# Gate and up projections multiplied in blocks: seven block products in place of eight, from the third chunk of inner features on

## The chip, the cores and the metric

The kernel runs on one core of one Trainium2 chip. A core has a matmul engine (PE, whose weight loads are listed as PEld), a vector engine (DVE), a scalar engine (ACT), a general engine (POOL) and a queue engine (SP), and each works through its own instructions in order; they meet at semaphores. Operands lie in an on-chip memory of 128 partitions (SBUF), and matmul results in 8 accumulator banks of 128 by 512 fp32 values (PSUM). The metric is the time of one execution in device microseconds (us): 2798.61 before, the median of 3 runs that lie between 2798.51 and 2798.78.

## The reference

A decoder trunk of 2 layers, over 512 tokens of 1024 features. Each layer is a gated feed-forward block (FFN), a block of three parallel token mixers, and a second FFN. The change touches the first half of the four FFNs only, the products with `w_gate` and `w_up`:

```
D_MODEL = 1024;  SEQ = 512;  DEPTH = 2;  D_FF = 2816
def swiglu(x, w_gate, w_up, w_down):
    return (jax.nn.silu(x @ w_gate) * (x @ w_up)) @ w_down
...
y = swiglu(rms_norm(h, ffn1_pre_g[l]), ffn1_w_gate[l], ffn1_w_up[l], ffn1_w_down[l])
h = h + MACARON_WEIGHT * rms_norm(y, ffn1_post_g[l])
```

All is fp32, and the kernel keeps nearly that precision: every operand of a matmul is split into a rounded part and the remainder, and three matmuls (hi by hi, hi by lo, lo by hi) make one product.

## The kernel before

**The products.** The normalised input stands transposed in SBUF as `xhi` and `xlo`, 8 blocks of 128 features by 512 tokens each. The 2816 inner features are worked off in 11 chunks of 256. For each chunk `load` (L220) brings 1 MB of `w_gate` and 1 MB of `w_up` into two staging buffers `ws`, one each, so a chunk's load waits until the last reader of the same matrix's earlier chunk is done. `part` and `split` (L201, L202) make the two halves of a piece of weights: ACT casts the rounded part `wh`, then DVE subtracts it from the weights to leave `wl`. There are three buffers each for `wh` and `wl`, of 128 by 1024.

**A chunk.** The first chunk of each FFN is multiplied the other way round: a tile of 128 tokens is the stationary operand and 256 columns of weights stream through (`gate_up`, its first loop). Meanwhile the last token tiles of the stage before are still being normalised and transposed into `xhi`, `xlo` (`spread`, called through `catch_up`). From the second chunk on weights are stationary and 512 tokens stream. Each 128 inner features take 8 feature blocks by 3 matmuls for gate and as many for up, so one chunk is 2 x 2 x 8 x 3 = 96 matmuls of 512 columns (`mm3`, L244 to L246). Then ACT applies silu to the gate sums (L1094) and DVE multiplies by the up sums (L1095) into `hid`, which `down` splits and multiplies with `w_down`.

**What sets the order.** A scheduler orders the instructions of each engine when the program is built; at run time each engine takes its own list strictly in order. Pools rotate: 7 buffers of 128 by 512 (`t`), 4 of 128 by 1024 (`m`), the three of `wh` and `wl`, and 8 banks.

The two functions that the diff touches, and what calls them:

Of the kernel before, what the change touches and what calls it, by code (L numbers as in the profile page):

```python
# [11 lines left out]
F32 = mybir.dt.float32  # L12
F32R = mybir.dt.float32r
I32 = mybir.dt.int32
AF = mybir.ActivationFunctionType
# [5 lines left out]
P = 128  # L21
# [4 lines left out]
KD = D // P  # L26
# [24 lines left out]
for _n, _k in (("ident", P), ("tri", P), ("ones64", P), ("ones", P),  # L51
# [8 lines left out]
BANKS = {"pj": (0, 1), "a": (2, 3, 4), "z": (5,), "n": (6,), "y": (7,), "all": tuple(range(8)),  # L60
         "t0": (0, 1), "t1": (2, 3), "t2": (4, 5), "t3": (6, 7)}

PUMP = {
# [35 lines left out]
class Core:  # L101
# [137 lines left out]
        for s in range(cols // P):  # L239
            yield self.part(st[:, :, s * P:(s + 1) * P])  # L240

    def mm3(self, out, whi, wlo, xhi, xlo, start, stop):
        nc = self.nc
        nc.tensor.matmul(out, whi, xhi, start=start, stop=False)  # L244
        nc.tensor.matmul(out, whi, xlo, start=False, stop=False)  # L245
        nc.tensor.matmul(out, wlo, xhi, start=False, stop=stop)  # L246

    def proj(self, ps, w, xhi, xlo, kc=KD):
        wh, wl = w
# [811 lines left out]
class Trunk(Rwkv, Hgrn, Mla, Core):  # L1061
    def gate_up(self, l, n):
        nc = self.nc
        hid = Lazy(lambda i: self.slot((0, 1, 2, 5, 8, 9)[i]))
        wg, wu = self.a[f"ffn{n}_w_gate"][l], self.a[f"ffn{n}_w_up"][l]

        g, u = self.first or (self.load(wg, KD, 256), self.load(wu, KD, 256))
        self.first = None
        gs = [self.part(g[:, 4 * i:4 * i + 4]) for i in range(2)]
        us = [self.part(u[:, 4 * i:4 * i + 4], (10, 9 if n == 1 else 7)[i]) for i in range(2)]  # L1070
        for t in range(NT):
            tk = slice(t * P, (t + 1) * P)
            ps = self.psum(f"t{t}", (P, 2, 256))
            for i, w in enumerate((gs, us)):
                for k in range(KD):
                    n = KD // len(w)
                    wh, wl = w[k // n]
                    self.mm3(ps[:, i], self.xhi[:, k, tk], self.xlo[:, k, tk], wh[:, k % n], wl[:, k % n], k == 0, k == KD - 1)
            sg = self.t2(shape=(P, 256))
            nc.scalar.activation(sg, ps[:, 0], AF.Silu)  # L1080
            nc.vector.tensor_mul(sg, sg, ps[:, 1])  # L1081
            ps = self.psum(f"t{t}", (P, 2, P))
            for i in range(2):
                self.transpose(ps[:, i], sg[:, i * P:(i + 1) * P])
            nc.scalar.copy(hid[0][:, 0:2, tk], ps)
            self.catch_up()
        for c in range(1, FF // 256):
            for s, (g, u) in enumerate(zip(self.columns(wg, KD, 256, col0=c * 256), self.columns(wu, KD, 256, col0=c * 256))):
                f = 2 * c + s
                pg, pu = self.psum("all"), self.psum("all")  # L1090
                self.proj(pg, g, self.xhi, self.xlo)
                self.proj(pu, u, self.xhi, self.xlo)
                sg = self.t2()
                nc.scalar.activation(sg, pg, AF.Silu)  # L1094
                nc.vector.tensor_mul(hid[f // 4][:, f % 4, :], sg, pu)  # L1095
        return hid


    def rows(self, acc, half, t, w, x, first, last):
# [209 lines left out]
```

## Time and profile before

| | |
|---|---|
| median of 3 runs | 2798.61 us |
| the profiled execution's own time | 2810.86 us |
| its span, first to last instruction | 2809.0 us |
| PE busy, share of the span | 2761.9 us, 98% |
| DVE busy | 1365.5 us, 49% |
| ACT busy | 1165.5 us, 41% |
| mean granted PE clock | 0.989 |
| HBM traffic over the span | 109 GB/s |

The profiled execution takes 12 us longer than the median of the plain runs. Its rows give durations and distances within it. Matmul rows overlap: the time from the start of one to the start of the next is what one costs in a stream, and the row's own length is longer. A row's columns in the timeline are start, length, engine, line, operation, operands (result before the arrow), and the idle time before it with what ended it. In rows of groups, the count stands after x, then busy us in total and the mean ns of one.

### The profile page before, as it was taken

Reading aid. Unit: us, or ns where it says so; the run is one execution under the profiler, and the core shown is the slowest. Engines: PE = TensorE matmul, PEld = TensorE weight load, DVE = VectorE, ACT = ScalarE, POOL = GpSimd, SP = SyncE. Lnnn points to the kernel's source line nnn. Section 1 sums busy time; section 2 is a strip of 40 time slices with the busy share of each in tenths; the row PEclk is TensorE's granted clock in tenths of the full one; section 3 lists DMA queues with packets and bytes.
Section 4 is the critical chain, followed back from the end, with each engine's and each line's share of the span. In section 5 each row is a group of like instructions: output and inputs, shape, how many; then the busy total and the mean of one; then the engine's idle time right before and its main releaser. Section 6 shows DMA issues by size and latency. Waiting matters only on the chain. (4 is left out here: it accounts for less than half of the span.)

```text
span 2809.0 us, 36592 instructions
## 1 busy us (share of the span) xinstructions
PE 2761.9 (98%) x15077; PEld 2271.6 (81%) x15077; DVE 1365.5 (49%) x2075; ACT 1165.5 (41%) x1901; POOL 59.0 (2%) x121
## 2 busy tenths in 40 slices
PE   8999999989999999999999999999899999999999
PEld 7888887777887888888888888877778878888887
DVE  3223347763866662223432233467558576522333
ACT  3223347345657542222332233364465584422232
POOL 0000010000000010000000000100000000100000
PEclk9999999899999999999999999999999999999999
DMA  4322332324421552322313233333253325323322
GB/s 164 103 97 92 119 118 94 104 70 160 147 79 63 173 176 83 105 90 98 127 63 103 90 105 112 103 106 103 83 195 102 106 68 179 131 90 97 102 102 75
DMA packets 223490, 307.32 MB, mean 109 GB/s; under 512 B 11856, under 2 KB 181052, under 8 KB 221788
## 3 DMA queue, kind: packets, MB, share of 16 engines
q1 hardware_dynamic: 223324, 304.99, 32.8%
q8 instruction: 118, 1.93, 0.3%
q14 instruction: 48, 0.39, 0.0%
HBM read 269.84 MB, written 35.13 MB: 109 GB/s over the span
## 5 line engine op out<-in xcount | busy, mean ns | idle before, releaser
L201 ACT CAST wh<-ws 128x1024 fp32r<-128x1024 f32 (+4 forms) x484 | 431.8, 902 | 1144.7 <-PE b L245 853.8
L246 PE MATMUL b<-xhi,wl 128*128 128x512 f32 x2176 | 857.8, 394 | 0.0
L244 PE MATMUL b<-xhi,wh 128*128 128x512 f32 x2176 | 856.8, 394 | 0.0
L245 PE MATMUL b<-xlo,wh 128*128 128x512 f32 x2176 | 856.2, 393 | 0.0
L202 DVE TENSOR_TENSOR wl<-ws,wh 128x1024 fp32r<-128x1024 f32 (+4 forms) x484 | 497.8, 1037 | 543.2 <-ACT wh L201 533.3
L244 PEld LDWEIGHTS b<-xhi,wh 128*128 128x128 f32 x2176 | 410.4, 189 | 89.8 <-issue 5.1
L246 PEld LDWEIGHTS b<-xhi,wl 128*128 128x128 f32 x2176 | 410.6, 189 | 87.4 <-issue 3.0
L245 PEld LDWEIGHTS b<-xlo,wh 128*128 128x128 f32 x2176 | 410.5, 189 | 86.1 <-issue 3.2
L244 PE MATMUL b<-wh,t 128*128 128x512 f32 x576 | 227.3, 395 | 0.0
L245 PE MATMUL b<-wl,t 128*128 128x512 f32 x576 | 227.3, 395 | 0.0
L246 PE MATMUL b<-wh,t 128*128 128x512 f32 x576 | 227.3, 395 | 0.0
L1095 DVE TENSOR_TENSOR s<-t,b 128x512 f32<-128x512 f32 x80 | 55.1, 688 | 265.9 <-PE b L246 265.9
L202 DVE TENSOR_TENSOR t<-s,t 128x512 fp32r<-128x512 f32 x80 | 54.6, 691 | 176.6 <-PE b L245 169.1
L245 PEld LDWEIGHTS b<-wl,t 128*128 128x128 f32 x576 | 108.5, 188 | 25.5
L246 PEld LDWEIGHTS b<-wh,t 128*128 128x128 f32 x576 | 108.5, 188 | 25.4
L244 PEld LDWEIGHTS b<-wh,t 128*128 128x128 f32 x576 | 108.5, 188 | 25.1
L244 PE MATMUL b<-s,wh 128*128 128x512 f32 x256 | 100.1, 391 | 0.0
L245 PE MATMUL b<-s,wh 128*128 128x512 f32 x256 | 99.6, 389 | 0.0
L246 PE MATMUL b<-s,wl 128*128 128x512 f32 x256 | 99.6, 389 | 0.0
L244 PE MATMUL b<-s,s 128*128 128x512 f32 x192 | 75.6, 394 | 0.0
L246 PE MATMUL b<-s,s 128*128 128x512 f32 x192 | 74.9, 390 | 0.0
L245 PE MATMUL b<-s,s 128*128 128x512 f32 x192 | 74.8, 390 | 0.0
(304 smaller groups left out, 3393.1 us busy)
## 6 DMA issues: line engine op xcount, KB each, us to landing
ws<-in_w_in_dram SPq DMA_DIRECT2D x58, 1024.0 KB
ws<-in_ffn_w_up_dram SPq DMA_DIRECT2D x44, 1024.0 KB
ws<-in_ffn_w_down_dram SPq DMA_DIRECT2D x44, 1024.0 KB
ws<-in_ffn_w_gate_dram SPq DMA_DIRECT2D x43, 1024.0 KB
gd<-f SPq DMA_DIRECT2D x48, 256.0 KB
t<-gd SPq DMA_DIRECT2D x48, 256.0 KB
s<-cd SPq DMA_DIRECT2D x8, 1024.0 KB
ws<-in_w_o_dram SPq DMA_DIRECT2D x8, 1024.0 KB
```

The costliest lines, as they stand in the source:

```text
L201: self.nc.scalar.copy(hi, src)
L202: self.nc.vector.tensor_sub(lo, src, hi.bitcast(F32))
L244: nc.tensor.matmul(out, whi, xhi, start=start, stop=False)
L245: nc.tensor.matmul(out, whi, xlo, start=False, stop=False)
L246: nc.tensor.matmul(out, wlo, xhi, start=False, stop=stop)
L1095: nc.vector.tensor_mul(hid[f // 4][:, f % 4, :], sg, pu)
```

## The change

From the third chunk on, a chunk is treated as a product of two 2 by 2 block matrices. The input is cut by tokens (two halves of 256) and features (two halves of 512): A11, A12, A21, A22, where A12 is the first token half with the second feature half. The weights are cut by features, with gate and up side by side: `b11` and `b21` are the upper and lower half of the gate columns, `b12` and `b22` those of the up columns. Strassen's scheme, in the form with 7 products and shared sums, gives gate and up of both token halves from seven block products. Each has 512 features, 256 inner features and 256 tokens: 2 x 4 x 3 = 24 matmuls of 256 columns, so a chunk has 7 x 24 = 168 of these in place of 96 of 512.

Sums of input blocks are formed once per FFN, in `token_sums`: 8 DVE additions or subtractions and 4 splits, all of 128 by 1024; S1, S2 and S4 go into slots of their own and S3 overwrites the block A21. Per chunk `seven` adds 4 subtractions of weight blocks on DVE (t1, t2, t3, and t2 again), splits seven pieces of weights in place of four, copies three banks to SBUF on ACT, adds three results and multiplies two on DVE, and takes two silus on ACT.

```diff
+PLAIN = 2
...
         for c in range(1, FF // 256):
-            for s, (g, u) in enumerate(zip(self.columns(wg, KD, 256, col0=c * 256), self.columns(wu, KD, 256, col0=c * 256))):
...
+            if c < PLAIN:
...
+            else:
+                if c == PLAIN:
+                    A = self.token_sums()
+                self.seven(A, self.load(wg, KD, 256, col0=c * 256), self.load(wu, KD, 256, col0=c * 256),
+                           hid[c // 2][:, 2 * (c % 2):2 * (c % 2) + 2, :])
         return hid
+
+    def token_sums(self):
+        nc = self.nc
+        U = (slice(0, 256), slice(256, 512))
+        at = lambda i, j: (self.xhi[:, 4 * j:4 * j + 4, U[i]], self.xlo[:, 4 * j:4 * j + 4, U[i]])
+        whole = lambda hi, lo: (hi.bitcast(F32), lo.bitcast(F32))
+        S = {"A11": at(0, 0), "A12": at(0, 1), "A22": at(1, 1)}
+        a, b, c = [self.m4((P, 4, 256)) for _ in range(3)]
+        add, sub = nc.vector.tensor_add, nc.vector.tensor_sub
+        add(a, *whole(*at(1, 0)))
+        add(b, *whole(*at(1, 1)))
+        add(b, a, b)
+        add(c, *whole(*at(0, 0)))
+        sub(a, c, a)
...
+        put("S1", 6, b)
+        sub(b, b, c)
+        put("S2", 7, b)
+        add(c, *whole(*at(0, 1)))
+        sub(c, c, b)
+        put("S4", 10, c)
+        self.split(*at(1, 0), a)
+        S["S3"] = at(1, 0)
+        return S
+
+    def seven(self, S, g, u, dst):
+        nc = self.nc
+        b11, b21, b12, b22 = g[:, 0:4], g[:, 4:8], u[:, 0:4], u[:, 4:8]
+        sub = nc.vector.tensor_sub
+        ps = [self.psum("all", (P, 2, 256)) for _ in range(3)]
+        started = set()
+
+        def product(i, w, x):
+            wh, wl = self.part(w)
+            xh, xl = S[x]
+            for s in range(2):
+                f = slice(s * P, (s + 1) * P)
+                for k in range(4):
+                    self.mm3(ps[i][:, s], wh[:, k, f], wl[:, k, f], xh[:, k], xl[:, k], i not in started, s == 1 and k == 3,
+                             skip_group_check=True)
+                    started.add(i)
+
+        def keep(i):
+            x = self.t2(shape=(P, 2, 256))
+            nc.scalar.copy(x, ps[i])
+            return x
+
+        product(0, b11, "A11")
+        t1, t2, t3 = [self.m4((P, 4, 256)) for _ in range(3)]
+        sub(t1, b12, b11)
+        p1 = keep(0)
+        product(1, t1, "S1")
+        sub(t2, b22, t1)
+        p5 = keep(1)
+        product(0, t2, "S2")
+        v = keep(0)
+        sub(t3, b22, b12)
+        product(2, b21, "A12")
+        nc.vector.tensor_add(p1, p1, ps[2])
+        nc.scalar.activation(p1, p1, AF.Silu)
+        product(0, t3, "S3")
+        nc.vector.tensor_add(p5, p5, ps[0])
+        product(1, b22, "S4")
+        nc.vector.tensor_add(v, v, ps[1])
+        nc.vector.tensor_mul(dst[:, :, 0:256], p1, v)
+        sub(t2, b21, t2)
+        product(0, t2, "A22")
+        sg = self.t2(shape=(P, 2, 256))
+        nc.scalar.activation(sg, ps[0], AF.Silu)
+        nc.vector.tensor_mul(dst[:, :, 256:512], sg, p5)
```

**How rows move.** A program lists each engine's instructions in the order in which the engine takes them. Names are those of the buffers: `wh`, `wl` the halves of a piece of weights, `ws` the staged weights, `m` a sum of weight blocks, `t` a buffer of 128 by 512, `b` a bank, `s` a slot (here a part of `hid`). In the changed kernel L205 is the second half of a split, L1167, L1170, L1174 and L1183 the four subtractions of weights, L1181 the addition that completes an up result, L1182 and L1187 the two multiplications into `hid`.

DVE in the middle of an FFN, one chunk before:

```order
L202 TENSOR_TENSOR wl_688<-ws_685,wh_687 128x1024
L202 TENSOR_TENSOR wl_694<-ws_691,wh_693 128x1024
L1095 TENSOR_TENSOR s_82_622<-t_682,b_88_633 128x512
L202 TENSOR_TENSOR wl_751<-ws_685,wh_750 128x1024
L202 TENSOR_TENSOR wl_755<-ws_691,wh_754 128x1024
L1095 TENSOR_TENSOR s_82_622<-t_747,b_97_698 128x512
```

and the first 12 of the 16 instructions of a chunk now (the other four are the split of `b22`, L1176, the split of the seventh piece, and L1179):

```order
L205 TENSOR_TENSOR wl_1262<-ws_1254,wh_1261 128x1024
L1167 TENSOR_TENSOR m_1289<-ws_1256,ws_1254 128x1024
L1181 TENSOR_TENSOR t_1130<-t_1130,b_136_1035 128x512
L1170 TENSOR_TENSOR m_1290<-ws_1256,m_1289 128x1024
L1182 TENSOR_TENSOR s_134_1033<-t_1069,t_1130 128x2x256
L205 TENSOR_TENSOR wl_1296<-m_1289,wh_1295 128x1024
L205 TENSOR_TENSOR wl_1327<-m_1290,wh_1326 128x1024
L1187 TENSOR_TENSOR s_134_1033<-t_1251,t_1100 128x2x256
L1174 TENSOR_TENSOR m_1291<-ws_1256 128x1024
L205 TENSOR_TENSOR wl_1358<-ws_1254,wh_1357 128x1024
L1183 TENSOR_TENSOR m_1290<-ws_1254,m_1290 128x1024
L205 TENSOR_TENSOR wl_1388<-m_1291,wh_1387 128x1024
```

Splits of the next chunk (`ws_1254`) now stand between the additions and multiplications that finish the chunk before it (`b_136_1035`, `s_134_1033`).

ACT where the gate and up products of an FFN end and `down` begins. Before, with the last silu at L1094 and the first two splits of `hid` behind it:

```order
L201 CAST wh_1743<-ws_1709 128x1024
L1094 ACTIVATE t_1694<-b_219_1644 128x512
L201 CAST t_1715<-s_47_262 128x512
L201 CAST t_1747<-s_47_262 128x512
L201 CAST t_1781<-s_47_262 128x512
```

and now, with the last silu at L1186:

```order
L204 CAST wh_2615<-ws_2613 128x1024
L204 CAST wh_2647<-ws_2613 128x1024
L204 CAST wh_2681<-ws_2679 128x1024
L1186 ACTIVATE t_2598<-b_294_2381 128x512
L204 CAST t_2619<-s_47_262 128x512
L204 CAST t_2651<-s_47_262 128x512
```

In both, the splits of `hid` that `down` needs first stand behind a silu. That silu reads the bank of the last-but-one product before (the gate product, with the up product still to follow), and the bank of the last product now. The same rows stand at this place in all four FFNs.

DVE in the second FFN, from the last token tile's transposes (`xlo`) to the third chunk; before:

```order
L202 TENSOR_TENSOR xlo_81<-b_1338_8500,xhi_80 128x4x128
L1081 TENSOR_TENSOR t_8556<-t_8556,b_1339_8507 128x256
L202 TENSOR_TENSOR wl_8628<-ws_8625,wh_8627 128x1024
L202 TENSOR_TENSOR wl_8685<-ws_8619,wh_8684 128x1024
L1081 TENSOR_TENSOR t_8612<-t_8612,b_1342_8563 128x256
L202 TENSOR_TENSOR wl_8689<-ws_8625,wh_8688 128x1024
```

and now (L1117 to L1131 are additions of `token_sums`, L1084 is the multiplication that was L1081):

```order
L205 TENSOR_TENSOR xlo_81<-b_1434_9404,xhi_80 128x4x128
L1117 TENSOR_TENSOR m_9649<-xhi_80,xlo_81 128x1024
L1118 TENSOR_TENSOR m_9650<-xhi_80,xlo_81 128x1024
L1120 TENSOR_TENSOR m_9651<-xhi_80,xlo_81 128x1024
L1119 TENSOR_TENSOR m_9650<-m_9649,m_9650 128x1024
L1121 TENSOR_TENSOR m_9649<-m_9651,m_9649 128x1024
L1084 TENSOR_TENSOR t_9460<-t_9460,b_1435_9411 128x256
L205 TENSOR_TENSOR s_1460_9657<-m_9650,s_1460_9657 128x1024
L205 TENSOR_TENSOR wl_9532<-ws_9529,wh_9531 128x1024
L1129 TENSOR_TENSOR m_9650<-m_9650,m_9651 128x1024
L205 TENSOR_TENSOR wl_9589<-ws_9523,wh_9588 128x1024
L1131 TENSOR_TENSOR m_9651<-xhi_80,xlo_81 128x1024
```

Five additions of the token sums now stand between the last `xlo` and the third tile's multiplication, and further sums between the splits of the second chunk's weights. Outside the four gate and up stages and their borders, the lists of all engines read as before. On SP one thing moves: the loads of the gain vectors for the norms behind the FFN (512 KB each, into `m` buffers, L264 now) stood ahead of most gate and up loads and now stand behind the last of them, just ahead of the first load of `w_down`.

More of the change, by code (lines that the diff above doesn't have):

```diff
@@ L240, in columns, with mm3 @@
             yield self.part(st[:, :, s * P:(s + 1) * P])
-    def mm3(self, out, whi, wlo, xhi, xlo, start, stop):
+    def mm3(self, out, whi, wlo, xhi, xlo, start, stop, **kw):
         nc = self.nc
-        nc.tensor.matmul(out, whi, xhi, start=start, stop=False)
-        nc.tensor.matmul(out, whi, xlo, start=False, stop=False)
-        nc.tensor.matmul(out, wlo, xhi, start=False, stop=stop)
+        nc.tensor.matmul(out, whi, xhi, start=start, stop=False, **kw)
+        nc.tensor.matmul(out, whi, xlo, start=False, stop=False, **kw)
+        nc.tensor.matmul(out, wlo, xhi, start=False, stop=stop, **kw)
     def proj(self, ps, w, xhi, xlo, kc=KD):
@@ L1087, in gate_up @@
         for c in range(1, FF // 256):
-            for s, (g, u) in enumerate(zip(self.columns(wg, KD, 256, col0=c * 256), self.columns(wu, KD, 256, col0=c * 256))):
[L1089 to L1095, printed above, removed]
@@ L1096, in gate_up @@
-        return hid
+            if c < PLAIN:
+                for s, (g, u) in enumerate(zip(self.columns(wg, KD, 256, col0=c * 256), self.columns(wu, KD, 256, col0=c * 256))):
+                    f = 2 * c + s
+                    pg, pu = self.psum("all"), self.psum("all")
+                    self.proj(pg, g, self.xhi, self.xlo)
+                    self.proj(pu, u, self.xhi, self.xlo)
+                    sg = self.t2()
+                    nc.scalar.activation(sg, pg, AF.Silu)
+                    nc.vector.tensor_mul(hid[f // 4][:, f % 4, :], sg, pu)
+            else:
[3 more added lines that the diff above has]
+                           hid[c // 2][:, 2 * (c % 2):2 * (c % 2) + 2, :])
@@ new lines, in gate_up, with put @@
+        return hid
+    def token_sums(self):
[11 more added lines that the diff above has]
+        sub(a, c, a)
+        def put(name, i, x):
+            both = self.slot(i, (P, 2, 4, 256), F32R)
+            self.split(both[:, 0], both[:, 1], x)
+            S[name] = both[:, 0], both[:, 1]
+        put("S1", 6, b)
[7 more added lines that the diff above has]
+        return S
```

## The prediction

> **What bounds the kernel now.** I read the page's first part and the waits of PE first.
>
> ```profile
> PE 2761.9 (98%) x15077; PEld 2271.6 (81%) x15077; DVE 1365.5 (49%) x2075; ACT 1165.5 (41%) x1901; POOL 59.0 (2%) x121
> ...
> PE b L516 <- DVE m L499: 16.7, 2, 8.5
> PE b L197 <- DVE m L282: 9.1, 3, 8.3
> PE b L197 <- DVE t L1081: 3.3, 3, 1.9
> ```
>
> PE is occupied nearly throughout, and its longest waits (us in total, times, longest) lie in the mixers (L516) and at the borders of stages. No wait of the gate and up chunks is among them. So these chunks cost what their matmuls cost, and DVE and ACT have room. The queue's own list gives the period of a chunk: each chunk issues one load of gate weights.
>
> ```profile
> 66.68 0.37 SPq L220 DMA_DIRECT2D ws<-in_ffn_w_gate_dram  x1
> 72.12 0.37 SPq L220 DMA_DIRECT2D ws<-in_ffn_w_up_dram  x1
> 88.44 0.37 SPq L220 DMA_DIRECT2D ws<-in_ffn_w_gate_dram  x1
> ...
> 131.96 0.37 SPq L220 DMA_DIRECT2D ws<-in_ffn_w_gate_dram  x1
> ```
>
> From 66.68 to 88.44 is 21.76 us, and from 66.68 to 131.96 three times that. A chunk has 96 matmuls, so one costs 21.76/96 = 226.7 ns. The timeline shows the same spacing, start to start, also while ACT and DVE split weights beside it:
>
> ```profile
> 102.42 1.05 ACT L201 CAST wh<-ws 128x1024 fp32r<-128x1024 f32 x1 [4.38 <-PE b L245]
> 102.45 0.39 PE L244 MATMUL b<-xhi,wh 128*128 128x512 f32 x1
> 102.67 0.39 PE L245 MATMUL b<-xlo,wh 128*128 128x512 f32 x1
> ...
> 103.51 1.23 DVE L202 TENSOR_TENSOR wl<-ws,wh 128x1024 fp32r<-128x1024 f32 x1 [4.21 <-ACT wh L201]
> ...
> 104.49 0.39 PE L244 MATMUL b<-xhi,wh 128*128 128x512 f32 x1
> ```
>
> Nine matmuls start between 102.45 and 104.49: 2.04/9 = 226.7 ns. The row's own 0.39 us is latency and overlaps the next row.
>
> **The matmuls after the change.** The question is what a matmul of 256 columns costs; half of 226.7 would be 113.3. The first chunk of each FFN runs such a stream already, with a 128 by 128 weight load for each matmul and the same three-matmul pattern:
>
> ```profile
> 30.29 0.28 PE L246 MATMUL b<-wh,xlo 128*128 128x256 f32 x1
> ...
> 30.31 0.38 ACT L1080 ACTIVATE t<-b 128x256 f32<-128x256 f32 x1 [1.00 <-PE b L246]
> ...
> 30.73 0.42 DVE L1081 TENSOR_TENSOR t<-t,b 128x256 f32<-128x256 f32 x1 [2.34 <-ACT t L1080]
> ...
> 31.01 0.28 PE L246 MATMUL b<-wh,xlo 128*128 128x256 f32 x1
> ...
> 33.28 0.28 PE L244 MATMUL b<-s,xhi 128*128 128x256 f32 x1
> 33.28 0.19 PEld L245 LDWEIGHTS b<-s,xhi 128*128 128x128 f32 x1
> ...
> 36.16 0.28 PE L244 MATMUL b<-wh,xhi 128*128 128x256 f32 x1
> ```
>
> From 33.28 to 36.16 are 24 starts: 120.0 ns each; from 30.29 to 31.01, with ACT and DVE at work, six at 120 too. So 512 columns cost 226.7 and 256 cost 120.0: 256 columns of streaming are 106.7 and each matmul has a fixed 13.3 on top. Seven eighths of the multiplications therefore cost 168 x 0.120 = 20.16 us a chunk and not 7/8 of 21.76 (19.04). **A chunk gains 1.60 us**, and nine chunks in each of four FFNs gain 36 x 1.60 = **57.6 us**. No gain is left where the spacing exceeds 21.76/168 = 129.5 ns, so there are 9.5 ns of room.
>
> The Trainium skill, page "TensorE: Matmul & The Clock Gate", section "Back-to-back issue gap", has two rules here. For a matmul alone it gives columns/2.4 + 2.5 ns: by it a chunk would go from 96 x 215.8 = 20.7 to 168 x 109.2 = 18.3 us, and the sum would gain 85. For a stream of weight loads and matmuls it gives 81 ns at 128 columns and 131 at 512; taking 98 between them as an estimate, a chunk would go from 12.6 to 16.4 us, and the change would cost 139 us. This case's 226.7 ns at 512 columns agrees with neither, and the second speaks against the change; the rows decide.
>
> **DVE and ACT beside them.** The rows by form that price the new work:
>
> ```profile
> L202 DVE TENSOR_TENSOR wl<-ws,wh 128x1024 fp32r<-128x1024 f32 x364 | 444.6, 1224 | 510.8 <-ACT wh L201 502.8
> L1095 DVE TENSOR_TENSOR s<-t,b 128x512 f32<-128x512 f32 x80 | 55.1, 688 | 265.9 <-PE b L246 265.9
> L201 ACT CAST wh<-ws 128x1024 fp32r<-128x1024 f32 x364 | 382.6, 1052 | 1074.6 <-PE b L245 785.8 <-PE b L246 251.3 <-issue 15.7
> L201 ACT CAST t<-s 128x512 fp32r<-128x512 f32 x80 | 48.5, 616 | 0.0
> L256 ACT COPY f<-b 128x512 f32<-128x512 f32 x82 | 47.5, 580 | 4.9 <-issue 4.4 <-PE b L246 0.3
> L1094 ACT ACTIVATE t<-b 128x512 f32<-128x512 f32 x80 | 47.3, 592 | 0.0
> ```
>
> DVE had 4 splits and 2 multiplications a chunk, 6.3 us. It gets 7 splits, 4 subtractions and 5 operations of 512: 11 x 1.224 + 5 x 0.688 = 16.9 us, 84% of 20.16. ACT gets 7 x 1.052 + 3 x 0.580 + 2 x 0.592 = 10.3 us. Both fit beside PE in sum; whether they fit in order needs DVE's list. I count from the end of the fifth product (S3) of a chunk. DVE then adds (0.69), splits the next chunk's b11 (1.22), forms t1 (1.22), adds v (0.69; its product ended at 2.88), forms t2 (1.22), multiplies (0.69) and splits t1 (1.22): 6.9 us. PE has three products of 24 x 0.12 = 2.88 us to do until it takes t1, at 8.6. The reserve is 1.7 us, the smallest of the seven; t2 comes at 8.1 for 11.5. So a steady chunk loses nothing by it; the price if the cover goes is under the rivals.
>
> **Weights.** The next loads may start when `b21` and `b22` were read last. From t1's subtraction to the split of b22 DVE has 9 operations of 1.224 and 3 of 0.688, 13.1 us. A load needs, by the windows around the issues at 66.68 and 72.12 (last two columns: share of the DMA engines, GB/s):
>
> ```profile
> 66.00:68.00 2.00, 2.00 (x11) 1.65 (x10) 0.65 (x1) 0.00 (x0) 0.00 (x0) 1.00 0.11 20
> 68.00:70.00 2.00, 2.00 (x10) 1.69 (x9) 0.00 (x0) 0.22 (x1) 0.00 (x0) 1.00 0.94 300
> 70.00:72.00 2.00, 2.00 (x10) 1.65 (x9) 1.13 (x1) 1.33 (x2) 0.00 (x0) 1.00 0.59 204
> 72.00:74.00 2.00, 2.00 (x11) 1.65 (x10) 0.09 (x1) 0.00 (x0) 0.00 (x0) 1.00 0.34 89
> ```
>
> The first ends before 72, so under 5.3 us. The loop is at most 18.4 of 20.16 us, closed with 1.8 to spare. The gain vectors that move on SP wait only for the last chunk's t1, which is split before `w_down` may load; I cost that at nothing.
>
> **Token sums.** 12 operations of 1.224 on DVE, 14.7 us an FFN. Uncovered they would cost 4 x 14.7 = 59 us, all of the gain. Their cover, in the second FFN:
>
> ```profile
> 1059.80 1.29 DVE L202 TENSOR_TENSOR xlo<-b,xhi 128x512 fp32r<-128x512 f32 x2 [0.16 <-ACT xhi L201]
> 1066.28 0.42 DVE L1081 TENSOR_TENSOR t<-t,b 128x256 f32<-128x256 f32 x1 [5.20 <-ACT t L1080]
> ...
> 1072.39 0.42 DVE L1081 TENSOR_TENSOR t<-t,b 128x256 f32<-128x256 f32 x1 [1.05 <-ACT t L1080]
> ```
>
> Inputs are whole at 1061.1, and the third chunk starts one chunk (21.8) after about 1072, at 1094: 33 us. DVE has 12 sums and splits, the second chunk's 4 splits, and for the third chunk 2 splits and 3 subtractions: 21 x 1.224, with small ones 28 us. They fit. But five sums now stand ahead of the third tile's multiplication, which starts at 1067.2, not 1066.28, and more ahead of the fourth, which slips to 1073.8 (five more operations of 1.224 behind 1067.6). PE's list lets nine matmuls of the second chunk (2 us) pass before that tile's transposes. Between 0 and 1.5 us an FFN I take **0.5, in all 2 us**.
>
> **The way into `down`.** Now the splits of `hid` that `down` takes first stand on ACT behind the silu of the last product. Before:
>
> ```profile
> 255.75 0.59 ACT L1094 ACTIVATE t<-b 128x512 f32<-128x512 f32 x1
> 256.24 1.65 ACT L201 CAST t<-s 128x512 fp32r<-128x512 f32 x3
> ```
>
> those casts were done by 257.9, and `down` began at 260.21 without a gap:
>
> ```profile
> 259.98 0.40 PE L246 MATMUL b<-xhi,wl 128*128 128x512 f32 x1
> 260.21 0.40 PE L244 MATMUL b<-wh,t 128*128 128x512 f32 x1
> ```
>
> Now PE ends its last product, ACT needs 0.59 for the silu and 0.62 for the cast, with some 0.15 for the result to reach ACT (latency 0.28 against a spacing of 0.12): 1.36 us in which PE has nothing else in its list. The remainder that DVE forms is needed seven matmuls later (1.6 us) and ready by then. Bounds 0.6 and 3 us; I take 1.36, **four times 5.4 us**.
>
> **Sum.** 57.6 - 2 - 5.4 = 50 us less. The profiled execution would go from its span of 2809.0 to 2759 (2810.86 to 2761); the gain is PE time in a stream, so the plain median goes from 2798.6 to **2748**.
>
> **Rivals.** *DVE's list sets the chunk, slower.* Its 16.9 us leave 3.3 idle in a chunk, and five of its sixteen operations wait for a result of PE or ACT, with the next chunk's splits queued behind. If it must stand for more than 21.76 - 16.9 = 4.9 us a chunk, nothing is gained. Two waits as long as a product, 5.8, give 22.7 us: 36 x 0.9 = 32 us more, with the borders 2838. One wait of 4.1 us gives 21.0, 30 us lost, and 2778. For it speaks the 84%, against it the reserves above: each result is ready when DVE comes to it.
>
> *Weight loads no longer hide, slower.* A load row lasts 0.19 us and the stream gives it 0.12, so loads overlap. If they did not when ACT and DVE load the memory, 168 x 0.19 = 31.9 us a chunk and a time near 3171; it decides from 129.5 ns on. Against it: 120 in rows with ACT and DVE busy, if lightly. (The stream rule of the Trainium skill's page "TensorE: Matmul & The Clock Gate" points the same way.)
>
> *The fixed part vanishes.* 113.3 ns, 36 x 2.72 = 98 us, about 2708. Nothing in the first chunk speaks for it. (The same page's rule for a matmul alone, with its 2.5 ns, comes near this one.)
>
> *The token sums are not covered.* 59 us lost, no change: 2799. Against it the 33 us of cover.
>
> **How the numbers follow.** Forecast 0.78, around 2748; DVE in part, near 2778, 0.08; DVE in full, 2838, 0.05; loads that don't hide 0.03; no fixed part 0.03; no change 0.03. Under the forecast alone 2740 (no losses at the borders, 57.6 gained) to 2760. To hold eight in ten I take 2738 to 2780, upwards because the unpriced part, DVE at 84%, can only cost. A measurement of this kernel tells 0.2% (5.6 us) from no change: faster 0.89, same 0.03, slower 0.08.
>
> **What would show it.** Gate loads 20.16 us apart in the steady chunks; matmul starts 120 ns apart there; DVE busy about 16.9 us of each chunk, yet no PE wait for a split; a PE gap of 1 to 2 us ahead of `down`, ended by ACT's cast; mixers unchanged. Wrong would be a spacing above 125 ns, PE waits for `wl` or `wh` in each chunk, or a gap of several us where the third chunk begins.

## The result, and the profile after

| | median, us | runs | profiled execution (span) | mean granted clock |
|---|---|---|---|---|
| before | 2798.68 | 2798.51 to 2798.78 | 2810.86 (2809.0) | 0.989 |
| after | 2751.32 | 2750.68 to 2752.31 | 2752.31 (2750.4) | 0.992 |

The ratio is 0.983, 95% interval [0.981, 0.984]: the change saves 47.4 us, and 2748 (50 us less) had been predicted, in a range of 2738 to 2780. The profiled spans differ by more, 58.6 us. A part of that is the clock. One minus the mean clock, times the span, is 30.9 us of lost cycles before and 22.0 after; the stretches at half clock that make the difference lie in the mixers, which the change doesn't touch (the longest, 27.3 us from 532.9 us on, stands in the execution before only).

The page of after begins with the busy times:

```profile
PE 2695.3 (98%) x17669; PEld 2341.1 (85%) x17669; DVE 1773.3 (64%) x2483; ACT 1347.5 (49%) x2133; POOL 58.5 (2%) x121
```

PE has 2592 matmuls more and is busy 66.6 us less. DVE has 408 us more to do, almost all of it beside PE. Whether that holds chunk by chunk is read from the queue's own list (one gate load a chunk) and from windows cut at two of these loads. Window columns: the stretch and its length, then busy time and instructions of PE, PEld, DVE, ACT and POOL, granted clock, DMA share, GB/s.

```profile
1097.78 0.37 SPq L223 DMA_DIRECT2D ws<-in_ffn_w_gate_dram  x1
1117.94 0.37 SPq L223 DMA_DIRECT2D ws<-in_ffn_w_gate_dram  x1
1138.11 0.37 SPq L223 DMA_DIRECT2D ws<-in_ffn_w_gate_dram  x1
...
1198.58 0.37 SPq L223 DMA_DIRECT2D ws<-in_ffn_w_gate_dram  x1
```

```profile
1097.78:1117.94 20.16, 20.16 (x171) 20.16 (x170) 16.06 (x16) 9.83 (x13) 0.00 (x0) 1.00 0.33 105
1117.94:1138.11 20.17, 20.17 (x171) 20.17 (x170) 16.07 (x16) 9.84 (x13) 0.00 (x0) 1.00 0.33 106
```

Six loads stand between 1097.78 and 1198.58, five steps of 20.16 us, as forecast, and PE is busy in every one of those microseconds at full clock. The waits of PE, by total:

```profile
PE b L519 <- DVE m L502: 16.6, 2, 8.5
PE b L200 <- DVE m L285: 9.0, 4, 8.1
PE b L247 <- ACT t L204: 8.1, 4, 2.0
PE b L200 <- DVE t L1084: 2.9, 3, 1.9
```

The mixers' wait (L519, before L516) is as it was, and so is the one ahead of the first chunk (L200 for L285). The wait for the first chunk's multiplication (L1084, before L1081), which the token sums were to make longer, went from 3.3 us to 2.9. No wait of a steady chunk is in the list. One row is new: four times 2.0 us for ACT's cast `t`. That is the way into `down`. Here it is in the first FFN, PE and ACT together:

```profile
245.25 0.28 PE L248 MATMUL b<-xlo,wh 128*128 128x256 f32 x1
245.37 0.28 PE L249 MATMUL b<-xhi,wl 128*128 128x256 f32 x1
245.57 1.04 ACT L204 CAST wh<-ws 128x1024 fp32r<-128x1024 f32 x1 [1.78 <-PE b L248]
246.52 0.59 ACT L1186 ACTIVATE t<-b 128x512 f32<-128x512 f32 x1
247.01 1.13 ACT L204 CAST t<-s 128x512 fp32r<-128x512 f32 x2
247.67 0.50 PE L247 MATMUL b<-wh,t 128*128 128x512 f32 x1 [2.02 <-ACT t L204]
```

From PE's last matmul of the stage (245.37) to the first of `down` (247.67) are 2.30 us. Before, that step was 0.23 (259.98 to 260.21 in the prediction's rows), so it is 2.07 us longer. Against the 0.12 that a stream of 256 columns gives it, each border costs 2.18 us, where 1.36 had been counted. The row that was not counted is the third one: a cast of weights for `down` that waits 1.78 us and stands ahead of the silu.

After the gap the clock fell in two of the four FFNs. Windows at the start of `down` in the first and the second FFN:

```profile
248.50:251.90 3.40, 3.40 (x10) 2.64 (x9) 2.98 (x5) 2.18 (x4) 0.00 (x0) 0.50 0.30 123
1255.40:1258.90 3.50, 3.50 (x10) 2.75 (x9) 3.13 (x6) 2.18 (x4) 0.00 (x0) 0.51 0.35 145
```

At a clock of 0.50, 3.4 us hold half of the matmuls that they could. `down` took 101.81 and 102.21 us in these two FFNs by its matmul starts, 100.25 in the other two, and 100.16 in all four before: 3.7 us in sum for the two.

Why two of four can be read from the kept traces. Seven traces, this one and those of six experiments below, have this gap, in 28 places, and half clock followed at 15 of them; at the 24 ways into `down` of the six traces without it (the kernel before among them) it never did. In each trace the half-clock stretches begin at whole multiples of 3.413 us from one another (the two here 1006.93 us, 295 times 3.4133). Divide the execution into such intervals: at the 15 places 1.88 to 2.02 us of the gap lie in the one interval ahead of the half clock, at the 13 others the border of two intervals cuts the gap and neither holds more than 1.85. So the gap brings the half clock, and where it happens to lie on that grid decides whether it does.

### The profile page after: what moved, and what is told of

It reads as the page before. It is cut to its first block, busy times and chain, and to the rows that moved or that the text cites. A ratio compares the mean times of both kernels' runs of the same rounds, so it can differ in the third digit from the quotient of the medians.

```text
span 2750.4 us, 42564 instructions
## 1 busy us (share of the span) xinstructions
PE 2695.3 (98%) x17669; PEld 2341.1 (85%) x17669; DVE 1773.3 (64%) x2483; ACT 1347.5 (49%) x2133; POOL 58.5 (2%) x121
## 5 line engine op out<-in xcount | busy, mean ns | idle before, releaser
L249 PE MATMUL b<-xhi,wl 128*128 128x256 f32 (+1 forms) x2176 | 734.0, 337 | 0.0
L247 PE MATMUL b<-xhi,wh 128*128 128x256 f32 (+1 forms) x2176 | 734.0, 337 | 0.0
L248 PE MATMUL b<-xlo,wh 128*128 128x256 f32 (+1 forms) x2176 | 732.6, 337 | 0.0
L204 ACT CAST wh<-ws 128x1024 fp32r<-128x1024 f32 (+4 forms) x448 | 393.5, 889 | 676.8 <-PE b L248 295.8
L205 DVE TENSOR_TENSOR wl<-ws,wh 128x1024 fp32r<-128x1024 f32 (+4 forms) x448 | 453.2, 1021 | 271.0 <-ACT wh L204 265.9
L247 PEld LDWEIGHTS b<-xhi,wh 128*128 128x128 f32 x2176 | 414.7, 191 | 45.2 <-issue 4.9
L248 PEld LDWEIGHTS b<-xlo,wh 128*128 128x128 f32 x2176 | 414.9, 191 | 40.8 <-issue 2.6
L247 PE MATMUL b<-s,wh 128*128 128x256 f32 (+1 forms) x1120 | 344.6, 308 | 0.0
L248 PE MATMUL b<-s,wh 128*128 128x256 f32 (+1 forms) x1120 | 344.2, 307 | 0.0
L249 PE MATMUL b<-s,wl 128*128 128x256 f32 (+1 forms) x1120 | 344.1, 307 | 0.0
L204 ACT CAST wh<-m 128x1024 fp32r<-128x1024 f32 x144 | 151.3, 1050 | 232.4 <-PE b L248 98.1
L248 PE MATMUL b<-wl,t 128*128 128x512 f32 x576 | 228.6, 397 | 0.0
L247 PEld LDWEIGHTS b<-s,wh 128*128 128x128 f32 x1120 | 213.9, 191 | 10.9 <-DVE s L991 1.2
L249 PEld LDWEIGHTS b<-s,wl 128*128 128x128 f32 x1120 | 213.9, 191 | 10.1
L248 PEld LDWEIGHTS b<-s,wh 128*128 128x128 f32 x1120 | 214.0, 191 | 9.8
L205 DVE TENSOR_TENSOR wl<-m,wh 128x1024 fp32r<-128x1024 f32 x144 | 173.8, 1222 | 34.2 <-ACT wh L204 34.2
L205 DVE TENSOR_TENSOR t<-s,t 128x512 fp32r<-128x512 f32 x80 | 54.9, 690 | 176.9 <-PE b L248 158.9
```

Of the source, the lines that this page charges most:

```text
L204: self.nc.scalar.copy(hi, src)
L205: self.nc.vector.tensor_sub(lo, src, hi.bitcast(F32))
L247: nc.tensor.matmul(out, whi, xhi, start=start, stop=False, **kw)
L248: nc.tensor.matmul(out, whi, xlo, start=False, stop=False, **kw)
L249: nc.tensor.matmul(out, wlo, xhi, start=False, stop=stop, **kw)
```

## Experiments

The theory after the comparison (Theory 1): PE alone sets the chunks, with 120 ns for a matmul of 256 columns whatever stands beside it; DVE's added work lies beside PE until DVE is full (after t3 was formed three times this became: what counts is that each result is ready when PE takes it, which depends on the place of an operation in DVE's list); what was lost is the border into `down`, where PE waits for ACT. Rivals: the 120 ns hold a loss by DVE's and ACT's load on the memory; DVE's sum of work is what limits; the border has little part in the missing microseconds.

| kernel | median, us | ratio to before, 95% interval |
|---|---|---|
| after | 2751.3 | 0.983 [0.981, 0.984] |
| first split of `hid` ahead of the last product | 2742.7; again 2742.2 | 0.980 [0.978, 0.982]; 0.980 [0.978, 0.982] |
| the kernel before, products in two halves of 256 columns | 2845.2 | 1.016 [1.015, 1.018] |
| scheme from the seventh chunk on | 2777.1 | 0.992 [0.990, 0.994] |
| without the subtractions of weights | 2758.2 | 0.984 [0.981, 0.987] |
| t3 three times (2 more DVE operations a chunk) | 2767.3 | 0.989 [0.987, 0.990] |
| t1 three times (2 more) | 2797.1 | 0.999 [0.997, 1.001] |
| 2 more behind the split of `b22` | 2753.7 | 0.984 [0.982, 0.987] |
| t3 five times (4 more) | 2902.2 | 1.036 [1.033, 1.040] |
| scheme from the second chunk on, with the border edit | 2744.8 | 0.980 [0.978, 0.982] |
| the kernel before, four quarters of 128 columns | 3558.5 | 1.270 [1.266, 1.274] |

**The border.** The first split of `hid` is written ahead of the last product, so that it no longer stands in ACT's list behind the last silu. `ahead` is `first_splits` in the last chunk of an FFN and nothing in the others; `chunk`, in `down`, takes what is ready:

```diff
+    def first_splits(self, hid):
+        self.ready = {}
+        for j in range(1):
+            hh, hl = self.t2(F32R), self.t2(F32R)
+            self.split(hh, hl, hid[j // 4][:, j % 4, :])
+            self.ready[j] = hh, hl
...
+        ahead()
         sub(t2, b21, t2)
         product(0, t2, "A22")
...
         def chunk(j, n):
+            if j in self.ready:
+                return self.ready.pop(j)
             if n < 0:
```

> One edit at the border of the gate and up stage: the split of the first piece of hid that the down products need is written ahead of the last block product, so it no longer stands behind the last silu on ACT. Theory 1 (PE's stream sets the chunk; the border gap of 2.30 us, 2.07 more than before, is ACT's list, and the half-clock stretches of 3.4 us behind two of the four gaps follow from the gap): four times 2.07 = 8.3 us and about 3.7 us of half clock go, near 2740 us, no half-clock stretch at the start of down. Rival (the half clock comes from elsewhere): 2743 with the stretches still there. Rival (something else, such as the banks or the weights, holds down back as long): no change, 2751.

Measured: 2742.7 us. The same kernel once more:

> The changed kernel with hid's first split ahead of the last product, once more and in more rounds. 2741 to 2744, a gain of 56 to 58 us over the kernel before and of 8 to 10 over the change.

Measured: 2742.2. PE's list of waits now has nothing between these rows:

```profile
PE b L519 <- DVE m L502: 16.8, 2, 8.6
PE b L200 <- DVE m L285: 8.7, 3, 8.0
PE b L200 <- DVE t L1084: 2.9, 3, 1.9
PE b L734 <- ACT t L958: 2.7, 2, 1.3
```

and `down` begins with the spacing of a stream, here in the second of the two runs:

```profile
245.94 0.28 PE L249 MATMUL b<-xhi,wl 128*128 128x256 f32 x1
246.06 0.39 PE L247 MATMUL b<-wh,t 128*128 128x512 f32 x1
```

Here ACT's weight cast still waits until 246.14, beside `down`, and costs nothing: PE has work whose inputs don't come through it. No half clock follows, and `down` takes 100.15 to 100.7 us. The border was worth 8.6 and 9.1 us of the median, against 8.7 us of waiting (4 x 2.18) and 3.7 of half clock in the one profiled execution. In medians this kernel beats both the kernel before and the change; single executions of it reach 2751, at a mean clock of 0.990 in place of 0.992 to 0.995, so it does not keep all of the 9 us each time.

**What a matmul costs, without the scheme.** The kernel before, each product of the steady chunks taken in pieces of the tokens; the multiplications and the work of DVE and ACT stay the same.

```diff
-                self.proj(pg, g, self.xhi, self.xlo)
-                self.proj(pu, u, self.xhi, self.xlo)
+                for ps, w in ((pg, g), (pu, u)):
+                    if c < 2:
+                        self.proj(ps, w, self.xhi, self.xlo)
+                        continue
+                    for h in (slice(0, 256), slice(256, 512)):
+                        for k in range(KD):
+                            self.mm3(ps[:, h], w[0][:, k, :], w[1][:, k, :], self.xhi[:, k, h], self.xlo[:, k, h], k == 0, k == KD - 1,
+                                     skip_group_check=True)
```

> The kernel before with nothing of the block scheme, but from the third chunk on each product runs in two token halves: 192 matmuls of 256 columns a chunk in place of 96 of 512, the same multiplications, no more work on DVE or ACT. Theory 1 (each matmul carries a fixed 13.3 ns whatever else runs): 192 x 0.120 = 23.04 us a chunk, 1.28 more than 21.76, 36 times: 46 us more than before, 2845. Rival (the fixed part belongs to the first chunk, or in the changed kernel to the busy DVE and ACT): 113.3 ns each, no change, 2799.

Measured: 2845.2, 1.6% more than before, or 45 us. The gate loads:

```profile
113.16 0.37 SPq L220 DMA_DIRECT2D ws<-in_ffn_w_gate_dram  x1
...
136.20 0.37 SPq L220 DMA_DIRECT2D ws<-in_ffn_w_gate_dram  x1
```

A chunk takes 23.04 us, 192 x 0.120 us; 36 of them instead of 21.76 make 46.1. So 120 ns hold also where DVE and ACT do no more than before: their load is no part of it. Then the same in quarters:

> The kernel before, but from the third chunk on each product runs in four token quarters: 384 matmuls of 128 columns a chunk. Theory 1 (a fixed 13.3 ns per matmul at every width): 53.3 + 13.3 = 66.7 ns each, 25.6 us a chunk, 138 us more than before, 2938. Rival (the weight load sets a floor somewhere under 120 ns, as the transposes of 128 columns with some 99 ns suggest): 38 us a chunk, 585 us more, 3385.

Measured: 3558.5. Theory 1 missed here: "a fixed 13.3 ns on top of the columns" would be 66.7 ns at 128 columns. The first and the last of sixteen starts in a row:

```profile
149.82 0.28 PE L246 MATMUL b<-xhi,wl 128*128 128x128 f32 x1
...
151.49 0.28 PE L246 MATMUL b<-xhi,wl 128*128 128x128 f32 x1
```

Fifteen steps in 1.67 us are 111.3 ns each, and the queue's loads agree:

```profile
110.14 0.37 SPq L220 DMA_DIRECT2D ws<-in_ffn_w_gate_dram  x1
153.02 0.37 SPq L220 DMA_DIRECT2D ws<-in_ffn_w_gate_dram  x1
195.90 0.37 SPq L220 DMA_DIRECT2D ws<-in_ffn_w_gate_dram  x1
```

42.88/384 = 111.7 ns. There is a floor of some 111.5 ns for a matmul that brings its own 128 by 128 weight load, and 256 columns lie only 8 ns above it. The rival named in the expectation, a floor by the load, has the direction right; it had taken 99 ns. The Trainium skill, page "TensorE: Matmul & The Clock Gate", section "LDWEIGHTS (loading the stationary operand)", gives a weight load columns/1.2, so 107 ns for 128 columns; the measured floor is 4% above that. That the loads make the floor fits both, though no run here took them away. A row of the mixers in the kernel before speaks for it, twelve matmuls whose load has 64 columns:

```profile
643.85 0.86 PE L584 MATMUL b<-t,s 64*64 64x64 f32 x12
```

One alone lasts 0.22, so they start (0.86 - 0.22)/11 = 58 ns apart, half of the floor at half of a load's columns. They stream fewer columns too (64), so this is a hint and no proof.

**Fewer chunks in the scheme.**

```diff
-PLAIN = 2
+PLAIN = 6
```

> The changed kernel with the block scheme from the seventh chunk on: 5 chunks in each FFN in place of 9. Theory 1 (1.58 us gained per chunk, about 2.4 us lost per FFN at the border, token sums hidden): 16 x 1.58 = 25 us slower than the changed kernel, 2776.6. Rival (no fixed loss per FFN, less gained per chunk: 47.4/36 = 1.32): 21 us slower, 2772.4. Rival (token sums cost several us per FFN, more gained per chunk): 2780 or more.

Measured: 2777.1. Going from 36 chunks in the scheme to 20 costs 25.8 us, 1.61 a chunk, and the border's wait is the same (`ACT t L204`, 8.1 us in four). The gain is proportional to the chunks, and what is lost is lost once an FFN.

**Without the subtractions.**

```diff
-        t1, t2, t3 = [self.m4((P, 4, 256)) for _ in range(3)]
-        sub(t1, b12, b11)
+        t1, t2, t3 = b12, b22, b21
-        sub(t2, b22, t1)
-        sub(t3, b22, b12)
-        sub(t2, b21, t2)
```

> The changed kernel without the four subtractions of weights in each chunk (products take the raw pieces, so the output is not the reference's): DVE has 16.06 - 4.88 = 11.2 us of work in a chunk of 20.16. Theory 1 (DVE lies wholly beside PE in the changed kernel, the shortfall against seven eighths is the matmuls' fixed part): no change against the changed kernel, 2751 to 2753. Rival (DVE already costs PE something in each chunk): up to 36 x 1.1 = 40 us less, if a chunk came down to 19.04.

Measured: 2758.2 in the median of 2764.0, 2752.5, 2750.9 and 2763.9. Nothing is gained by 4.9 us less DVE work a chunk. The median is even 7 us up, but not in the stages: by their matmul starts the four gate and up stages took 203.35 to 203.41 us, as in the change (203.35). The profiled execution, 2762.2 long, lost 33 us to the clock (0.988), 11 more than the change's, in the mixers.

**More work for DVE, at three places.** First t3 is formed three times:

```diff
-        sub(t3, b22, b12)
+        for _ in range(3):
+            sub(t3, b22, b12)
```

> The changed kernel with the third subtraction of weights done three times over, so two more operations of 1.22 us on DVE in each of the 36 chunks: 16.06 + 2.44 = 18.5 of 20.16 us. Theory 1 (DVE lies beside PE until it is full): no change, 2751, within 2 us. Rival (DVE's list and its waits already set the chunk, or its traffic slows PE): up to 36 x 2.44 = 88 us more; any rise above 5 us speaks for it.

Measured: 2767.3, 16 us more than the change. My theory as it stood (18.5 of 20.16 us still fit) missed. PE's waits, a chunk cut at two of this kernel's gate loads, and three matmuls of that chunk in a row show where:

```profile
PE b L249 <- DVE wl L205: 3.5, 9, 0.8
```

```profile
1142.80:1163.28 20.48, 20.47 (x171) 20.27 (x170) 18.22 (x19) 10.04 (x12) 0.00 (x0) 1.00 0.32 103
```

```profile
1146.04 0.28 PE L248 MATMUL b<-xlo,wh 128*128 128x256 f32 x1
1146.32 0.38 PE L249 MATMUL b<-xhi,wl 128*128 128x256 f32 x1
1146.54 0.28 PE L247 MATMUL b<-xhi,wh 128*128 128x256 f32 x1
```

The matmul that takes t3's `wl` comes 0.28 us behind the one before it and the next 0.22 behind it, where the stream has 0.12 each: 0.26 us, too short to be listed as a wait, in most chunks, and up to 0.8 of listed wait in nine. The four gate and up stages are so 11.6 us longer than the change's in the profiled executions. DVE is busy for 18.22 us of the chunk, so it stands for 2.26, and still comes too late for something: a full list is not what limits. Two theories are left: the place in the list, or a share of DVE from which losses begin wherever the work stands. Two kernels with exactly as much added work tell them apart, one with t1 formed three times instead,

```diff
-        sub(t1, b12, b11)
+        for _ in range(3):
+            sub(t1, b12, b11)
```

> The changed kernel with the subtraction t1 = b12 - b11 written three times in every chunk of the scheme (same values, two more DVE operations of 1.22 us a chunk, as many as where t3 was written three times, which gave 2767). Theory 1 (what decides is the place in DVE's list): these two stand ahead of the split of t1, where I counted a reserve of 1.7 us, so 2.45 us overdraw it by 0.8 us and more with the latencies between engines: 1.1 to 1.6 us a chunk, 40 to 57 us, 2791 to 2808, and PE waits for `wl` of the second product. Theory 2 (only DVE's sum of work decides, 19.4 of 20.16 us): the same as with t3 three times, 2767.

and one with two subtractions behind the split of `b22`:

```diff
                     started.add(i)
+            return wl.bitcast(F32)
...
-        product(1, b22, "S4")
+        wl = product(1, b22, "S4")
+        for _ in range(2):
+            sub(t3, wl, wl)
```

> The changed kernel with two more subtractions of the same size in every chunk (lo half of b22 minus itself, into t3's buffer, which nobody reads afterwards; values of the output unchanged). They stand in DVE's list just behind the split of b22 and the addition behind it, ahead of the split of the seventh piece. Theory 1 (the place decides): here DVE is ahead of PE by more than 2.45 us, so nothing is lost: 20.16 us a chunk, 2751. Theory 2 (DVE's sum decides): as with t3 three times, 2767.

Measured: 2797.1 and 2753.7. The same work costs 46 us at the one place, 16 at the second, and 2 at the third, which lies within the runs of the change and of this kernel (2750.5 to 2763.8). Windows of the third, and of t1 three times cut at two of its gate loads:

```profile
1097.78:1117.94 20.16, 20.16 (x170) 20.16 (x169) 18.02 (x19) 9.93 (x12) 0.00 (x0) 1.00 0.33 105
```

```profile
1175.49:1196.84 21.35, 20.42 (x171) 20.22 (x170) 18.21 (x19) 9.83 (x12) 0.00 (x0) 1.00 0.31 99
```

DVE is as busy in both (18.0 and 18.2 us); in the one PE never stands, in the other a chunk takes 21.35. The waits and DVE's list of the latter say why:

```profile
PE b L249 <- DVE wl L205: 31.8, 32, 1.2
```

```profile
1161.17 0.69 DVE L1180 TENSOR_TENSOR t<-t,b 128x512 f32<-128x512 f32 x1 [0.65 <-PE b L249]
...
1168.53 1.22 DVE L1171 TENSOR_TENSOR m<-ws,m 128x1024 f32<-128x1024 f32 x1
1169.67 1.22 DVE L205 TENSOR_TENSOR wl<-m,wh 128x1024 fp32r<-128x1024 f32 x1
```

From the addition behind the fifth product (L1180, ended by PE) to the split of t1 are 8.50 us. In the change the same two rows are 5.63 apart:

```profile
1146.18 0.69 DVE L1179 TENSOR_TENSOR t<-t,b 128x512 f32<-128x512 f32 x1 [0.65 <-PE b L249]
...
1151.81 2.37 DVE L205 TENSOR_TENSOR wl<-m,wh 128x1024 fp32r<-128x1024 f32 x2
```

The difference, 2.87, is two operations, which follow each other at 1.14 us, and the second multiplication (L1188, 0.60), which the program's order now puts ahead of the split. In the change the split ends at 1151.81 + 1.22 = 1153.03. PE begins t1's product there at 1154.62, so the reserve is 1.6 us as the prediction counted it (1.7), and takes the first `wl` with the third matmul, at 1154.86:

```profile
1154.86 0.28 PE L249 MATMUL b<-s,wl 128*128 128x256 f32 x1
```

So 1.83 us can go before PE waits, and 2.87 overdraws them by 1.04. The same place with t1 three times:

```profile
1169.73 0.28 PE L248 MATMUL b<-s,wh 128*128 128x256 f32 x1
1170.94 0.39 PE L249 MATMUL b<-s,wl 128*128 128x256 f32 x1 [0.93 <-DVE wl L205]
1171.17 0.28 PE L247 MATMUL b<-s,wh 128*128 128x256 f32 x1
```

The step to the waiting matmul is 1.21 and the one behind it 0.23, where the stream has 0.12 each: 1.20 us, and the chunk grew by 21.35 - 20.16 = 1.19. 36 times that are 43 of the 46 us; two chunks of the fourth FFN, shown below, lost more. That settles it for the place.

Then four operations more at t3's place:

```diff
-        sub(t3, b22, b12)
+        for _ in range(5):
+            sub(t3, b22, b12)
```

> The changed kernel with the third subtraction done five times over: four more operations of 1.22 us on DVE per chunk, 16.06 + 4.88 = 20.9 us. Two more had cost 0.35 us a chunk (2767) although DVE had 18.5 us of work in 20.16. Theory 2 (what decides is the place in DVE's list: the reserve behind that subtraction is some 2.6 us, of which each operation takes 1.22, and beyond it every operation adds its length because waits for PE stand in the list): 22.8 us a chunk, 36 x 2.65 = 95 us above the changed kernel, 2846, slower than before. Rival (DVE's sum decides): 20.9 us a chunk, 27 us above, 2779.

Measured: 2902.2, slower than the kernel before, and by more than any theory had it. Waits, and two chunks as windows:

```profile
PE b L247 <- ACT wh L204: 58.4, 36, 2.7
PE b L249 <- DVE wl L205: 20.4, 28, 0.8
```

```profile
1158.52:1182.98 24.46, 22.20 (x173) 21.79 (x171) 20.87 (x21) 9.70 (x12) 0.00 (x0) 0.93 0.27 87
1182.98:1208.68 25.70, 23.31 (x170) 22.80 (x169) 20.86 (x21) 9.70 (x12) 0.00 (x0) 0.87 0.25 82
```

PE waits 79 us in all, 2.2 a chunk (2.65 had been worked out). The rest is clock: in both chunks the granted clock is below 1, and over the execution it is 0.969, so 90 us of lost cycles against the change's 22. 79 + 68 = 147 of the 151 us, though the two overlap by some us where PE waits at half clock. A wait of up to 2.7 us in every chunk is paid for twice, once as a wait and once as half clock behind it. With t1 three times, where the waits are at most 1.3 us and mostly one a chunk, that is rare: two chunks, both in the fourth FFN, hold a stretch of half clock.

```profile
2541.99:2564.56 22.57, 20.68 (x158) 20.28 (x157) 18.23 (x18) 8.49 (x11) 0.00 (x0) 0.92 0.29 94
2608.75:2632.21 23.46, 20.96 (x161) 20.56 (x160) 18.21 (x18) 9.16 (x11) 0.00 (x0) 0.93 0.28 90
```

In these two a second wait stands less than 3 us ahead of the one for t1 (0.65 and 1.24 us, 1.26 and 1.24).

**One more chunk in the scheme.** The border edit, and the second chunk also in the scheme:

```diff
-PLAIN = 2
+PLAIN = 1
```

> The border edit, and the block scheme already from the second chunk on: ten chunks per FFN instead of nine, so the token sums lose the plain second chunk that covered them. Theory 1 (cover needed: about 15 us of sums and splits on DVE before the fifth product, 11 us of cover left): four chunks gain 6.3 us, stalls of 4 to 8 us per FFN outweigh it, 2750 to 2765 against 2741 with the border edit alone. Rival (the sums are needed late enough to be hidden anyway): 2736.

Measured: 2744.8, no gain over 2742.2 and no loss that shows, so neither of the two expectations came. By their starts the stages took 202.3 to 204.5 us, 203.8 on average, against 203.35: the 1.6 us that the tenth chunk gains, and 0.5 more, go back to the token sums, which are no longer covered by a plain chunk. The rows that are longer than with the border edit alone:

```profile
PE b L200 <- DVE t L1084: 4.5, 4, 1.9
PE b L249 <- DVE wl L205: 3.9, 3, 1.8
```

This is the price that the prediction gave the token sums if their cover went, but not its size: 15 us an FFN were named there and some 2 came, since the sums push only part of the splits past their due time.

## Why the prediction was right

| term | predicted, us | measured, us |
|---|---|---|
| 36 chunks | 57.6 | 57.6: 36 x (21.76 - 20.16) |
| token sums ahead of the third chunk | -2 | 0: the wait at L1084 went from 3.3 to 2.9 |
| way into `down` | -5.4 | -8.7 waiting (4 x 2.18), and -3.7 half clock in the profiled execution |
| sum | 50 | 45.2; the medians differ by 47.4 |

- *A chunk gains 1.60 us.* Held. The price of 120 ns, read from the first chunk of the kernel before, was the right one, and the halves showed that it doesn't depend on what runs beside PE. The explanation that I gave it was wrong in part: a fixed 13.3 ns is what 256 and 512 columns have in common, but it can't be carried to 128. The room of 9.5 ns that the prediction saw was real; that on the other side a floor stands 8 ns below, it had no row for.
- *DVE at 84%, smallest reserve 1.7 us at t1.* Held, and this was the step most worth testing. The reserve counted from DVE's list, 1.7, is 1.6 in the trace (1.8 up to the matmul that takes the split), and overdrawing it by 1.04 us cost 1.19 a chunk. The rival "DVE's list sets the chunk" was right as a mechanism (t1 three times takes the whole gain, 2797) and did not apply by a margin of about one and a half operations. Its bound "more than 4.9 us of standing" was not: 2.4 us of work at the wrong place were enough to lose all.
- *Loads of weights.* They come 20.16 us apart, in time. The loop's reserve was not tried.
- *Token sums.* The cover of 33 us held; they cost nothing, and the 2 us set aside were not needed. With one plain chunk less the cover begins to fail.
- *Way into `down`, 1.36 us.* This term was mis-sized: 2.18 us. The step that failed is "ACT needs 0.59 for the silu and 0.62 for the cast". In ACT's list a cast of weights (`wh`) stands just ahead of the silu; it stood in the rows that I had printed. I took it for done by then. But `wh` has three buffers, two of them hold the next pieces, and the third is the one that the last product reads, so the cast can't begin before that product ends (`[1.78 <-PE b L248]`), and it takes 0.95 us until the silu may start. The half clock behind the gap was not foreseen at all.
- *No fixed part, loads that don't hide, uncovered sums.* None came.

That 50 came within 3 us of the 47.4 is in part luck: the border cost 7 us more than its term, and the 2 us set aside for the sums and 2 us from elsewhere made up for more than half of it. These last 2 us of the median's gain are in no term. The first chunk's stretch of the four FFNs was 0.2 to 1.6 us shorter after, 2.8 in sum, by its matmul starts in one execution of each; why stays open.

## What to carry to other kernels

Price a matmul from a row with the same number of columns and the same weight load, not from the work it does: seven eighths of the products at half the width saved 7.3% of a chunk's time, not 12.5%, and the whole of the products at a quarter of the width took nearly twice the time (42.88 us a chunk against 21.76). For an engine beside the critical one, count the reserve at each result that PE takes, in the order of the list; the same two operations cost 46, 16 or 2 us here by their place alone. Where a stage ends with a chain through an engine that also prepares the next stage's weights, look for what in that engine's list waits for a buffer that the last product still holds, and give PE something to do meanwhile.

## What the runs showed of the hardware that I had not expected

- Matmuls with a weight load each start 226.7 ns apart at 512 columns, 120.0 at 256 and 111.5 at 128: below 256 columns hardly anything is gained.
- A gap of 2.0 us in PE was followed by 3.4 us at half clock at 15 of 28 places, those where at least 1.88 us of it lay in one interval of the 3.413 us grid. Waits of up to 2.7 us in every chunk were followed by a mean clock of 0.87 to 0.93, single waits of 1.2 us by none, and two such waits less than 3 us apart by half clock again, in one of the two cases with only 1.8 us of them in one interval. The Trainium skill, page "TensorE: Matmul & The Clock Gate", section "What's actually happening", has half rate set in after an idle window of about 3.4 us, whose phase is not tied to the program; the length of the slow stretch and the grid agree with that window, but the gaps that brought it here were shorter.
- DVE's rows of 1.22 us for 128 by 1024 follow each other at 1.14, and those of 0.69 at 0.60, when nothing is waited for; the busy time of a chunk is so 16.1 us where the sum of the rows gives 16.9.
